# The order of the chosen experts: per-partition lists written whole by two indirect DMAs in place of 128 scatters of single values

## Chip, cores and metric

One NeuronCore of a Trainium2 chip runs the whole program. The metric is the device time of one execution in microseconds, as a median of several runs. Shares and durations inside the execution come from one profiled execution.

## What is computed

The program runs two transformer-like blocks over 256 tokens of width 2048 in float32 (16 meta tokens go ahead of them in the first block). The part that matters here is the expert layer of the first block: 8 heads, 128 by 128 product keys, 16,384 experts, 16 experts for each token and head.

```python
v1, i1 = lax.top_k(s1, K); v2, i2 = lax.top_k(s2, K)
cand = (v1[..., :, None] + v2[..., None, :]).reshape(B, L, PH, K * K)
cidx = (i1[..., :, None] * NK + i2[..., None, :]).reshape(B, L, PH, K * K)
top_s, pos = lax.top_k(cand, K)
idx = jnp.take_along_axis(cidx, pos, axis=-1)
gate = jax.nn.softmax(top_s, axis=-1)
...
u = U[ib]
h = jax.nn.gelu(jnp.einsum('thkd,td->thk', u, xb).astype(jnp.float32), approximate=False)
w = (gb * h).astype(xb.dtype)
return jnp.einsum('thk,thkd->td', w, V[ib])
```

An expert that no token chose adds nothing to the sum, so rows of `V` need to be read only for the chosen ones. With the inputs that are used, the 32,768 choices of the 256 tokens fall on 13,426 different experts.

## The kernel before

**Stages around the change.** Expert number e = 128 i + p stands in partition p at place i. (1) The queries are projected, scored against the keys, and `choose` (lines 865 to 881) finds each token's experts, head by head, with VectorE. It is a background generator: `bg.tick()` lets it go a step each time a piece of TensorE's work has been traced. Each head adds 32 indirect DMAs on GpSimd's queue (line 836, 256 in all), each of which adds 128 gate values at single places of `table`, a DRAM tensor of 16,384 experts by 256 tokens. (2) Meanwhile `hidden(e2)` (lines 741 to 756) works through all 64 pairs e2 of 128-expert groups: two loads of `peer_u` of 1 MB on SyncE's queue, split by ScalarE (line 176) and VectorE (line 177) into a high and a low part for three matmul passes, 96 matmuls in a pair, then the activation and a store to the DRAM tensor `hid` on ScalarE's queue (lines 753 to 755). (3) After the choice `compact` (lines 940 to 983) counts the used experts with TensorE, gives each expert its place (used ones first, in order of their number) and writes the numbers to the DRAM tensor `order` with 128 indirect DMAs of 128 single values of 4 bytes (line 972). It then loads `order` as `rows` (line 981). (4) When all 64 pairs have been traced, `index_rows` (lines 985 to 997) turns `rows` with TensorE, so that partition p and column k hold the expert at place 128 k + p. (5) A conditional (line 1086) holds the work for the case of more than 106 x 128 = 13,568 used experts (`NS` = 106). Its body is a unit: each engine that has work in it loads the count, compares and branches, and nothing behind it is traced among the work ahead of it. (6) `weigh` (line 999) gathers gates (`gq` from `table`) and activations (`hq` from `hid`) of 2 x 128 places by four indirect DMAs and multiplies them. Five pairs of `weigh` and the projections of the memory's keys and values (`mem_w_kv`, lines 1095 to 1110) come first. Then 106 rows of 128 experts are taken one after the other: `v_row` (line 1021) gathers 128 rows of 8 KB of `peer_v`, and 24 matmuls add them up (line 1115 on), the next pair's `weigh` being traced in between.

**What sets the order.** TensorE's order is written by hand. The other engines' queues are ordered by a scheduler, roughly by the order of tracing. GpSimd's queue is served in order, so line 972 stands behind the 256 instructions of line 836. `peer_u` loads go through 4 slots of `raw`, the split halves through 4 slots, `gq` and `hq` through 2. `memory()` (line 886, the norm of the memory's rows) is background work that starts at pair `MEM` = 40.

Of the kernel before, what the change touches and what calls it, by code (L numbers as in the profile page):

```python
# [8 lines left out]
F32 = mybir.dt.float32  # L9
# [11 lines left out]
NT = 256  # L21
# [53 lines left out]
def _build(tc, nc, V, S, T, G, ctx, I, out):  # L75
# [265 lines left out]
    table = tc.dram_tile([128 * 128 * NT, 1], F32, name="table")  # L341
# [3 lines left out]
    def zeros(x):  # L345

        z = cst.tile([128, 128], F32, name="zero", tag="zero", bufs=1)
        V.tensor_scalar(z.bitcast(I32), x.bitcast(I32), 0, None, op0=OP.bitwise_and)  # L348
        nc.gpsimd.dma_start(table.rearrange("(q p a b) o -> q p a (b o)", q=16, p=128, b=128)[next(zq)],  # L349
                            z[:, None, :].to_broadcast([128, 16, 128]))  # L350

# [588 lines left out]
    def compact(cnt):  # L940


        ev = tkp.tile([128, NR], I32, name="ev", bufs=1)
        G.iota(ev, pattern=[[128, NR]], base=0, channel_multiplier=1)
        rev = tkp.tile([128, NR], F32, name="rev", bufs=1)
        V.tensor_scalar(rev, ev, -1.0, 128.0 * NR, op0=OP.mult, op1=OP.add)
        order = tc.dram_tile([128 * NR, 1], I32, name="order")
        put = []
        sums = [tkp.tile([128, 64 + NR], F32, name=f"sums{i}", bufs=1) for i in range(2)]
        for x in sums:  # L950
            V.memset(x[:, :64], 0.0)
        used = tkp.tile([128, NR], F32, name="used", bufs=1)
        V.tensor_scalar(used, cnt, 0.5, None, op0=OP.is_gt)
        V.tensor_copy(sums[0][:, 64:], used)
        for i in range(7):
            x, y = sums[i % 2], sums[1 - i % 2]
            V.tensor_add(y[:, 64:], x[:, 64:], x[:, 64 - (1 << i):64 + NR - (1 << i)])
# [3 lines left out]
        T.matmul(p[:, :NR], lhsT=triu, rhs=used, start=True, stop=False)  # L961
        T.matmul(p[:, :NR], lhsT=ones, rhs=sums[1][:, 63:63 + NR], start=False, stop=True)
        T.matmul(p[:, NR:NR + 1], lhsT=ones, rhs=sums[1][:, 63 + NR:64 + NR], start=True, stop=True)
        yield
        ids["n"] = ixp.tile([128, 1], I32, name="count")
        V.tensor_copy(ids["n"], p[:, NR:NR + 1])
        mq = tkp.tile([128, NR], F32, name="mq", bufs=1)
        V.scalar_tensor_tensor(mq, used, -1.0, rev, op0=OP.add, op1=OP.mult)
        pos = tkp.tile([128, NR], I32, name="pos", bufs=1)
        V.scalar_tensor_tensor(pos, p[:, :NR], -1.0, mq, op0=OP.add, op1=OP.subtract)  # L970
        for k in range(NR):
            d = G.indirect_dma_start(
                out=order, out_offset=bass.IndirectOffsetOnAxis(ap=pos[:, k:k + 1].bitcast(U32), axis=0),
                in_=ev[:, k:k + 1], in_offset=None)
            for d0 in put:
                tc.declare_no_dep(d.ins, d0.ins, reason="other places")
            put.append(d)
            if k % 32 == 31:
                yield
        rows = tkp.tile([128, 128], I32, name="rows", bufs=1)  # L980
        nc.gpsimd.dma_start(rows, order.rearrange("(b p) o -> b (p o)", p=128))
        ids["rows"] = rows
        yield

    def index_rows():

        of = tkp.tile([128, 128], F32, name="of", bufs=1)
        with tc.issue_after(mark["V"].ins):
            V.tensor_copy(of, ids["rows"])
        p = ptp()  # L990
        T.transpose(p[:, :NR], of, ident)
        ids["g"] = ixp.tile([128, NR], I32, name="ig")
        ids["v"] = ixp.tile([128, 2, NR], I32, name="iv")
        with tc.issue_after(mark["V"].ins):
# [73 lines left out]
    for e2 in range(NR // 2):  # L1068
# [7 lines left out]
        for _ in hidden(e2):  # L1076
            bg.tick()
# [644 lines left out]
```

## Time and profile before

| what | us |
|---|---|
| median of 3 runs | 3613.2 |
| lowest and highest run | 3604.57, 3615.6 |
| the profiled execution | 3621.4 |
| its span, first to last instruction | 3619.4 |
| TensorE busy in the span | 3469.8 (96%) |
| VectorE busy | 2370.8 (66%) |
| ScalarE busy | 1624.5 (45%) |
| GpSimd busy | 1153.5 (32%) |

TensorE is busy nearly throughout, so the time is TensorE's work plus the stretches in which it waits or runs at a lower granted clock. The profiled execution is 8.2 us longer than the median of the runs. A share of the whole span says little here: each stage has its own limit, and the stretches have to be read one by one.

### The profile page before, as it was taken

Reading aid. Unit: us, or ns where it says so; the run is one execution under the profiler, and the core shown is the slowest. Engines: PE = TensorE matmul, PEld = TensorE weight load, DVE = VectorE, ACT = ScalarE, POOL = GpSimd, SP = SyncE. Lnnn points to the kernel's source line nnn. Section 1 sums busy time; section 2 is a strip of 40 time slices with the busy share of each in tenths; the row PEclk is TensorE's granted clock in tenths of the full one; section 3 lists DMA queues with packets and bytes.
Section 4 is the critical chain, followed back from the end, with each engine's and each line's share of the span. In section 5 each row is a group of like instructions: output and inputs, shape, how many; then the busy total and the mean of one; then the engine's idle time right before and its main releaser. Section 6 shows DMA issues by size and latency. Waiting matters only on the chain. (4 is left out here: it accounts for less than half of the span.)

```text
span 3619.4 us, 54532 instructions
## 1 busy us (share of the span) xinstructions
PE 3469.8 (96%) x21755; PEld 3099.8 (86%) x21755; DVE 2370.8 (66%) x4316; ACT 1624.5 (45%) x2148; POOL 1153.5 (32%) x780
## 2 busy tenths in 40 slices
PE   8999999999999999999986499999999999999999
PEld 7988899888889999999976378877777899999987
DVE  6975579976559996655422355544456688888875
ACT  6444443445454443344322254443336645454543
POOL 0000000000006888888645536666640000000000
PEclk9999999999999999999988799999999999999999
DMA  4544445667666777767896476666665444444443
GB/s 161 173 152 140 142 138 188 219 210 257 231 210 164 202 196 201 204 196 233 173 151 91 172 256 229 233 225 211 223 213 171 146 155 158 155 162 146 158 162 112
DMA packets 351878, 662.05 MB, mean 183 GB/s; under 512 B 60033, under 2 KB 209765, under 8 KB 321906
## 3 DMA queue, kind: packets, MB, share of 16 engines
q1 hardware_dynamic: 256962, 472.68, 42.2%
q0 software_dynamic: 75232, 164.85, 15.9%
q10 hardware_dynamic: 19424, 20.98, 1.9%
q8 instruction: 173, 2.83, 0.3%
q14 instruction: 87, 0.71, 0.1%
HBM read 620.43 MB, written 37.99 MB: 182 GB/s over the span
## 5 line engine op out<-in xcount | busy, mean ns | idle before, releaser
L176 ACT CAST hi<-raw 128x1024 fp32r<-128x1024 f32 x1093 | 1142.7, 1049 | 1669.6 <-PE acc L208 568.2
L177 DVE TENSOR_TENSOR lo<-raw,hi 128x1024 fp32r<-128x1024 f32 x1093 | 1327.6, 1222 | 775.1 <-ACT hi L176 763.9
L206 PE MATMUL mm<-xh,hi 128*128 128x256 f32 x2064 | 595.3, 288 | 23.1 <-ACT hi L176 22.5
L836 POOL DMA_INDIRECT table<-gts,idx x256 | 573.2, 2239 | 135.5 <-issue 75.6
L206 PE MATMUL acc<-xh,hi 128*128 128x256 f32 (+1 forms) x2048 | 604.9, 295 | 0.7 <-DVE hg L428 0.7
L208 PE MATMUL mm<-xh,lo 128*128 128x256 f32 x2064 | 593.4, 288 | 10.0 <-DVE lo L177 8.8
L207 PE MATMUL mm<-xl,hi 128*128 128x256 f32 x2064 | 591.3, 286 | 0.4 <-issue 0.4
L208 PE MATMUL acc<-xh,lo 128*128 128x256 f32 (+1 forms) x2048 | 586.8, 287 | 0.0
L207 PE MATMUL acc<-xl,hi 128*128 128x256 f32 (+1 forms) x2048 | 586.6, 286 | 0.0
L206 PEld LDWEIGHTS mm<-xh,hi 128*128 128x128 f32 x2064 | 402.7, 195 | 25.8 <-ACT hi L176 24.9
L208 PEld LDWEIGHTS mm<-xh,lo 128*128 128x128 f32 x2064 | 402.4, 195 | 14.1 <-DVE lo L177 12.2
L207 PEld LDWEIGHTS mm<-xl,hi 128*128 128x128 f32 x2064 | 402.8, 195 | 0.9 <-issue 0.8
L206 PEld LDWEIGHTS acc<-xh,hi 128*128 128x128 f32 x2048 | 390.5, 191 | 5.4 <-issue 5.0
L207 PEld LDWEIGHTS acc<-xl,hi 128*128 128x128 f32 x2048 | 390.8, 191 | 1.4 <-issue 1.0
L208 PEld LDWEIGHTS acc<-xh,lo 128*128 128x128 f32 x2048 | 389.9, 190 | 1.3 <-issue 1.2
L349 POOL DMA_DIRECT2D table<-zero x16 | 18.0, 1122 | 975.1 <-DVE zero L348 953.5
L206 PE MATMUL acc<-hi,xh 128*128 128x512 f32 x704 | 280.3, 409 | 0.0
L207 PE MATMUL acc<-lo,xh 128*128 128x512 f32 x704 | 278.2, 395 | 0.0
L208 PE MATMUL acc<-hi,xl 128*128 128x512 f32 x704 | 277.8, 395 | 0.0
L437 DVE SCALAR_TENSOR_TENSOR h<-hg,cw,h 128x256 f32<-128x256 f32 x480 | 203.7, 480 | 0.0
L736 POOL DMA_INDIRECT gq<-table,ig x106 | 152.3, 1437 | 149.3 <-DVE hq L1009 121.8
L207 PE MATMUL acc<-lo,wh 128*128 128x512 f32 x424 | 170.3, 402 | 13.3 <-DVE lo L177 13.3
(521 smaller groups left out, 5751.4 us busy)
## 6 DMA issues: line engine op xcount, KB each, us to landing
raw<-in_peer_u_dram SPq DMA_DIRECT2D x128, 1024.0 KB
raw<-in_w_in_dram SPq DMA_DIRECT2D x112, 1024.0 KB
raw<-in_dn_w_in_dram SPq DMA_DIRECT2D x88, 1024.0 KB
raw<-in_w_out_dram SPq DMA_DIRECT2D x48, 1024.0 KB
raw<-in_w_gla_out_dram SPq DMA_DIRECT2D x16, 1024.0 KB
table<-zero POOLq DMA_DIRECT2D x16, 1024.0 KB
raw<-in_w_conv_out_dram SPq DMA_DIRECT2D x16, 1024.0 KB
raw<-in_peer_wq_dram SPq DMA_DIRECT2D x16, 1024.0 KB
```

Source lines behind the costliest of these rows:

```text
L176: S.copy(hi, src)
L177: V.tensor_sub(lo, src, hi)
L206: T.matmul(o, lhsT=lh, rhs=rh, start=start, stop=False)
L207: T.matmul(o, lhsT=lh, rhs=rl, start=False, stop=False)
L208: T.matmul(o, lhsT=ll, rhs=rh, start=False, stop=stop)
L349: nc.gpsimd.dma_start(table.rearrange("(q p a b) o -> q p a (b o)", q=16, p=128, b=128)[next(zq)], z[:, None, :].to_broadcast([128, 16, 128]))
L437: V.scalar_tensor_tensor(ca[:, f], hg[:, f - f0, j:j + NT], w, ca[:, f], op0=OP.mult, op1=OP.add)
L736: G.indirect_dma_start(out=dst, out_offset=None, in_=rows, in_offset=bass.IndirectOffsetOnAxis(ap=ids.bitcast(U32), axis=0))
L836: d = G.indirect_dma_start(out=table, out_offset=bass.IndirectOffsetOnAxis(ap=idx[:, i, s:s + 1].bitcast(U32), axis=0), in_=gts[:, i, s:s ...
```

## The change

`compact` no longer gives each expert a place by a running sum over columns. Each partition makes a list of its own used experts (number + 1, falling, zeros behind) by 16 rounds of the 8 greatest values with VectorE. The 128 lists, 128 values or 512 bytes each, are written whole to DRAM at element offsets which follow from the counts of the partitions ahead. Two indirect DMAs do this, one for partitions 0 to 63 and one for 64 to 127 (each writes the other half to a spare area), into two buffers that two earlier DMAs have filled with zeros. The partitions take turns (0, 64, 1, 65, ...), so that the zeros at a list's end meet only the other half's place, and the two buffers are added after the load. If two neighbours in that order have fewer than 128 used experts together, 32,768 is added to the count. `got` is loaded as 128 x 106 directly, so partition p holds places 106 p to 106 p + 105, and the turn with TensorE goes. Places without an expert point at row 16,384, a zero row which `table` gets in addition; `hid` and `peer_v` are read there at row 16,383 (`ids["h"]`).

The conditional's body no longer goes on from place 13,568: it works through all 64 pairs in natural order with plain loads on SyncE's queue (the order is then all zero rows). `index_rows` is traced after pair `IX` = 55 and not after pair 63, and `MEM` is 30 and not 40.

The diff, with the removed bodies of `compact` and `index_rows` left out (they are printed above):

```diff
@@ -338,7 +338,7 @@
         split_store(xh[:, k], xl[:, k], xs, pcol(N1, k))
     pn1.close()
-    table = tc.dram_tile([128 * 128 * NT, 1], F32, name="table")
+    table = tc.dram_tile([(128 * 128 + 1) * NT, 1], F32, name="table")
     zq = iter(range(16))
@@ -346,8 +346,11 @@
         z = cst.tile([128, 128], F32, name="zero", tag="zero", bufs=1)
         V.tensor_scalar(z.bitcast(I32), x.bitcast(I32), 0, None, op0=OP.bitwise_and)
-        nc.gpsimd.dma_start(table.rearrange("(q p a b) o -> q p a (b o)", q=16, p=128, b=128)[next(zq)],
+        q = next(zq)
+        nc.gpsimd.dma_start(table[:128 * 128 * NT].rearrange("(q p a b) o -> q p a (b o)", q=16, p=128, b=128)[q],
                             z[:, None, :].to_broadcast([128, 16, 128]))
+        if q == 0:
+            nc.gpsimd.dma_start(table[128 * 128 * NT:].rearrange("(p b) o -> p (b o)", p=2), z[:2])
     pgl = ctx.enter_context(ExitStack())
@@ -940,72 +943,118 @@
     def compact(cnt):
...
+        lists = [tc.dram_tile([257 * 128, 1], F32, name=f"lists{i}") for i in range(2)]
+        z = tkp.tile([128, 129], F32, name="zl", bufs=1)
+        V.memset(z, 0.0)
+        for x in lists:
+            nc.gpsimd.dma_start(x[:129 * 128].rearrange("(p b) o -> p (b o)", p=128), z)
+        ev = tkp.tile([128, 3, NR], I32, name="ev", bufs=1)
+        G.iota(ev[:, 0], pattern=[[128, NR]], base=1, channel_multiplier=1)
+        G.iota(ev[:, 1], pattern=[[1, NR]], base=0, channel_multiplier=0)
+        G.iota(ev[:, 2], pattern=[[0, NR]], base=0, channel_multiplier=1)
+        evf = tkp.tile([128, 3, NR], F32, name="evf", bufs=1)
+        V.tensor_copy(evf, ev)
+        late = tkp.tile([128, 2, NR], F32, name="late", bufs=1)
+        V.tensor_scalar(late, evf[:, 1:], 63.5, -127.0, op0=OP.is_gt, op1=OP.mult)
+        rank = evf[:, 1:]
+        V.scalar_tensor_tensor(rank, rank, 2.0, late, op0=OP.mult, op1=OP.add)
+        low = tkp.tile([128, 1], F32, name="low", bufs=1)
+        V.tensor_scalar(low, late[:, 1, 0:1], -63.5, None, op0=OP.is_gt)
+        far, ahead = late[:, 0], late[:, 1]
+        V.tensor_sub(far, rank[:, 1], rank[:, 0])
+        V.tensor_scalar(ahead, far, -1.0, 0.5, op0=OP.mult, op1=OP.is_gt)
+        both = tkp.tile([128, NR], F32, name="both", bufs=1)
+        V.tensor_scalar(both, far, 0.5, 0.25, op0=OP.subtract, op1=OP.mult)
+        V.tensor_mul(both, both, both)
+        V.tensor_scalar(both, both, -1.0, -0.05, op0=OP.mult, op1=OP.is_gt)
+        mid = tkp.tile([128, 1], F32, name="mid", bufs=1)
+        V.tensor_scalar(mid, rank[:, 1, 0:1], -1.0, -126.5, op0=OP.mult, op1=OP.is_gt)
+        yield
+        keys = [tkp.tile([128, NR], F32, name=f"keys{i}", bufs=1) for i in range(2)]
+        used = keys[1]
         V.tensor_scalar(used, cnt, 0.5, None, op0=OP.is_gt)
...
+        cn = tkp.tile([128, 2], F32, name="cn", bufs=1)
+        V.tensor_reduce(cn[:, 0:1], used, axis=AX.X, op=OP.add)
+        V.tensor_mul(keys[0], used, evf[:, 0])
+        own = tkp.tile([128, NR], F32, name="own", bufs=1)
+        yield
+        for r in range(NR // 8):
+            r8 = slice(r * 8, r * 8 + 8)
+            V.max(own[:, r8], keys[r % 2])
+            if r < NR // 8 - 1:
+                V.match_replace(keys[1 - r % 2], in_to_replace=own[:, r8], in_values=keys[r % 2], imm_value=0.0)
+            if r % 4 == 3:
+                yield
         p = pmm()
-        T.matmul(p[:, :NR], lhsT=triu, rhs=used, start=True, stop=False)
-        T.matmul(p[:, :NR], lhsT=ones, rhs=sums[1][:, 63:63 + NR], start=False, stop=True)
-        T.matmul(p[:, NR:NR + 1], lhsT=ones, rhs=sums[1][:, 63 + NR:64 + NR], start=True, stop=True)
-        yield
+        T.matmul(p[:, 0:1], lhsT=ahead, rhs=cn[:, 0:1], start=True, stop=True)
+        T.matmul(p[:, 1:2], lhsT=both, rhs=cn[:, 0:1], start=True, stop=True)
+        off = tkp.tile([128, 3], F32, name="off", bufs=1)
+        V.tensor_scalar(off[:, 1:2], tok[:, 0:1], 128.0, 129.0 * 128, op0=OP.mult, op1=OP.add)
+        V.tensor_sub(off[:, 0:1], p[:, 0:1], off[:, 1:2])
+        V.tensor_mul(off[:, 2:3], low, off[:, 0:1])
+        to = [tkp.tile([128, 1], I32, name=f"to{i}", bufs=1) for i in range(2)]
+        V.tensor_add(to[0], off[:, 2:3], off[:, 1:2])
+        V.tensor_sub(to[1], p[:, 0:1], off[:, 2:3])
+        few = tkp.tile([128, 1], F32, name="few", bufs=1)
+        V.tensor_scalar(few, p[:, 1:2], -1.0, -127.5, op0=OP.mult, op1=OP.is_gt)
+        V.tensor_scalar(few, few, mid[:, 0:1], 32768.0, op0=OP.mult, op1=OP.mult)
+        V.tensor_add(cn[:, 1:2], cn[:, 0:1], few)
+        for x in range(2):
+            G.indirect_dma_start(
+                out=lists[x].rearrange("(p b) o -> p (b o)", b=128),
+                out_offset=bass.IndirectOffsetOnAxis(ap=to[x].bitcast(U32), axis=1), in_=own, in_offset=None)
+        yield
+        yield
+        p = pmm()
+        T.matmul(p[:, 0:1], lhsT=ones, rhs=cn[:, 1:2], start=True, stop=True)
         ids["n"] = ixp.tile([128, 1], I32, name="count")
...
+        V.tensor_copy(ids["n"], p[:, 0:1])
+        fit = tkp.tile([128, 1], F32, name="fit", bufs=1)
+        V.tensor_scalar(fit, p[:, 0:1], -1.0, -128.0 * NS - 0.5, op0=OP.mult, op1=OP.is_gt)
+        got = tkp.tile([128, 2, NS], F32, name="got", bufs=1)
+        for x in range(2):
+            nc.gpsimd.dma_start(got[:, x], lists[x][:128 * NS].rearrange("(p k) o -> p (k o)", p=128))
+        ids["got"], ids["fit"] = got, fit
         yield
     def index_rows():
-        of = tkp.tile([128, 128], F32, name="of", bufs=1)
+        got, fit = ids["got"], ids["fit"]
         with tc.issue_after(mark["V"].ins):
...
+            V.tensor_add(got[:, 0], got[:, 0], got[:, 1])
+        V.tensor_scalar(got[:, 0], got[:, 0], fit[:, 0:1], None, op0=OP.mult)
+        V.tensor_scalar(got[:, 1], got[:, 0], 0.0, 128.0 * 128 + 1, op0=OP.is_equal, op1=OP.mult)
+        ex = tkp.tile([128, NS], F32, name="ex", bufs=1)
+        V.scalar_tensor_tensor(ex, got[:, 1], -1.0, got[:, 0], op0=OP.add, op1=OP.add)
+        ids["g"] = ixp.tile([128, NS], I32, name="ig")
+        V.tensor_copy(ids["g"], ex)
+        V.tensor_scalar(ex, ex, 128.0 * 128 - 1, None, op0=OP.min)
+        ids["h"] = ixp.tile([128, NS], I32, name="ih")
+        V.tensor_copy(ids["h"], ex)
+        ids["v"] = ixp.tile([128, 2, NS], I32, name="iv")
+        for k in range(2):
+            V.tensor_scalar(ids["v"][:, k], ex, 2.0, float(k), op0=OP.mult, op1=OP.add)
+    def weigh(e2, wp, ww, natural=False):
         wh = wp.tile([128, 2, NT], F32R, name="wh")
         wl = wp.tile([128, 2, NT], F32R, name="wl")
         gq = ww.tile([128, 2, NT], F32, name="gq")
         hq = ww.tile([128, 2, NT], F32, name="hq")
-        for e in range(2):
-            k = e2 * 2 + e
-            fetch(gq[:, e], table.rearrange("(e t) o -> e (t o)", t=NT), ids["g"][:, k:k + 1])
-            fetch(hq[:, e], hid, ids["g"][:, k:k + 1])
+        if natural:
+            es = slice(e2 * 2, e2 * 2 + 2)
+            nc.sync.dma_start(gq, table[:128 * 128 * NT].rearrange("(i p t) o -> p i (t o)", p=128, t=NT)[:, es])
+            nc.sync.dma_start(hq, hid.rearrange("(i p) t -> p i t", p=128)[:, es])
+        else:
+            for e in range(2):
+                k = e2 * 2 + e
+                fetch(gq[:, e], table.rearrange("(e t) o -> e (t o)", t=NT), ids["g"][:, k:k + 1])
+                fetch(hq[:, e], hid, ids["h"][:, k:k + 1])
         V.tensor_mul(hq, hq, gq)
         split_store(wh, wl, hq)
         return wh, wl
@@ -1021,7 +1070,7 @@
     def v_row(k):
         raw = load(None, [2, 1024])
-        fetch(raw.rearrange("p h f -> p (h f)"), Vv, ids["g"][:, k:k + 1])
+        fetch(raw.rearrange("p h f -> p (h f)"), Vv, ids["h"][:, k:k + 1])
         return raw
     def add_row(a, e, w, hi, lo, start, stop):
@@ -1064,7 +1113,7 @@
     pge = ctx.enter_context(ExitStack())
     gel = pge.enter_context(pool("gel", bufs=4))
-    MEM = 40
+    MEM, IX = 30, 55
     for e2 in range(NR // 2):
         if e2 == MEM:
             pme = ctx.enter_context(ExitStack())
@@ -1075,8 +1124,10 @@
             bg.add(memory(), 0.75)
         for _ in hidden(e2):
             bg.tick()
+        if e2 == IX:
+            bg.drain()
+            index_rows()
     bg.drain()
-    index_rows()
     pge.close()
     ptk.close()
     pwt = ctx.enter_context(ExitStack())
@@ -1084,11 +1135,12 @@
     pww = pwt.enter_context(ExitStack())
     ww = pww.enter_context(pool("wtw", bufs=2))
     with tc.If(nc.values_load(ids["n"][0:1, 0:1]) > NS * 128):
-        for e2 in range(NS // 2, NR // 2):
-            w = weigh(e2, wp, ww)
+        for e2 in range(NR // 2):
+            w = weigh(e2, wp, ww, True)
             for hf in range(2):
                 a = [[acc() for _ in range(2)] for _ in range(2)]
-                for e, hi, lo in halved(v_rows(e2, hf), 2, 1024):
+                rows = Vv.rearrange("(i p) f -> p i f", p=128)[:, e2 * 2:e2 * 2 + 2, hf * 1024:hf * 1024 + 1024]
+                for e, hi, lo in halved(load(rows, [2, 1024]), 2, 1024):
                     add_row(a, e, w, hi, lo, e == 0, e == 1)
                 take_values(a, hf)
     ws = [weigh(e2, wp, ww) for e2 in range(WA)]
```

## Rows read from the trace of the kernel before

**Rows 1.** The page's 40 slices: TensorE's busy tenths.
```profile
PE   8999999999999999999986499999999999999999
```

**Rows 2.** Stretches: busy PE, PEld, DVE, ACT, POOL; clock, DMA share, GB/s.
```profile
1190.00:1753.00 563.00, 562.69 (x4801) 561.68 (x4800) 378.39 (x637) 247.59 (x276) 495.93 (x220) 1.00 0.73 206
1753.00:1977.00 224.00, 186.79 (x1346) 179.50 (x1344) 74.53 (x84) 64.41 (x76) 118.26 (x107) 0.90 0.91 136
1977.00:2038.00 61.00, 1.27 (x2) 0.47 (x2) 2.01 (x5) 2.52 (x3) 29.04 (x32) 0.50 0.18 40
...
2135.00:2400.00 265.00, 264.89 (x1135) 213.30 (x1136) 140.22 (x141) 113.43 (x122) 163.54 (x140) 1.00 0.68 235
2400.00:2650.00 250.00, 236.71 (x992) 184.48 (x992) 118.86 (x123) 98.02 (x104) 161.13 (x124) 1.00 0.63 219
```

**Rows 3.** Tile order: count, ns min/median/max, first and last start.
```profile
L972 POOL DMA_INDIRECT order<-ev,pos x128: 952/958/1964, 1760.0 to 2015.2; - x128
L981 POOL DMA_DIRECT2D rows<-order x1: 587/587/587, 2023.2 to 2023.2; - x1
```

**Rows 4.** The same for line 836, the additions into table.
```profile
L836 POOL DMA_INDIRECT table<-gts,idx x256: 1542/2370/7091, 1108.8 to 1757.1; - x128
```

**Rows 5.** Waits, 1760 to 2030 us: who waited for whom, us, times, longest.
```profile
ACT hi L176 <- DMA raw<-in_peer_u_dram: 123.4, 21, 10.2
...
DVE of L989 <- DMA rows<-order: 49.2, 1, 49.2
```

**Rows 6.** DMA queues, 1300 to 1740 us: packets, MB, share of 16 engines.
```profile
q1 hardware_dynamic: 11033, 80.29, 53.5%
q0 software_dynamic: 24624, 0.10, 12.5%
```

**Rows 7.** DMA queues, 1780 to 1960 us.
```profile
q1 hardware_dynamic: 3067, 22.26, 88.5%
...
q0 software_dynamic: 2724, 0.05, 1.5%
```

**Rows 8.** Stores of the activated pairs from 1740 us on.
```profile
L755 ACTq DMA_DIRECT2D hid<-gel x16: 366/366/367, 1743.1 to 1977.6; - x16
```

**Rows 9.** VectorE's timeline, pairs 47 and 48: start, us, what.
```profile
1730.13 0.69 DVE L753 TENSOR_TENSOR gel<-mm,rB 128x512 f32<-128x512 f32 x1 [0.70 <-PE mm L208]
...
1741.65 0.69 DVE L753 TENSOR_TENSOR gel<-mm,rB 128x512 f32<-128x512 f32 x1 [0.69 <-PE mm L208]
```

**Rows 10.** Line 1086, the branch, by sequencer.
```profile
L1086 ACTq TENSOR_LOAD <-count x1: 470/470/470, 1978.0 to 1978.0; - x1
...
L1086 PEldq TENSOR_LOAD <-count x1: 491/491/491, 2026.3 to 2026.3; - x1
...
L1086 PEldq COMPARE_BRANCH  x1: 3361/3361/3361, 2026.9 to 2026.9; - x1
...
L1086 DVEq EVENT_SEMAPHORE  x1: 21/21/21, 2030.5 to 2030.5; - x1
```

**Rows 11.** The chain that ended last, behind the branch.
```profile
2030.62 5.11 DMA raw<-in_mem_w_kv_dram
...
2038.18 0.80 PE acc L207
```

**Rows 12.** VectorE's timeline among the chosen rows: two successive products.
```profile
2502.49 0.69 DVE L1009 TENSOR_TENSOR hq<-hq,gq 128x512 f32<-128x512 f32 x1 [6.16 <-DMA hq<-hid,ig]
...
2514.57 0.69 DVE L1009 TENSOR_TENSOR hq<-hq,gq 128x512 f32<-128x512 f32 x1 [6.25 <-DMA hq<-hid,ig]
```

**Rows 13.** GpSimd's timeline there: a pair's last activation gather.
```profile
2510.69 0.95 POOL L736 DMA_INDIRECT hq<-hid,ig  x1 [0.30 <-issue]
```

**Rows 14.** DMA, 2140 to 2700 us: gathers' queue, gathers of peer_v.
```profile
q0 software_dynamic: 23392, 123.58, 64.1%
...
raw<-in_peer_v_dram,ig POOLq DMA_INDIRECT x88
```

**Rows 15.** Groups on VectorE by shape, 1050 to 1800 us: busy us, mean ns.
```profile
L768 DVE MAX8 tv<-w 128x8 f32<-128x128 f32 x32 | 9.1, 285 | 0.0
```

More of the change, by code (lines that the diff above doesn't have):

```diff
@@ L940, in compact @@
     def compact(cnt):
[L943 to L951, printed above, removed]
@@ L952, in compact @@
-        used = tkp.tile([128, NR], F32, name="used", bufs=1)
-        V.tensor_scalar(used, cnt, 0.5, None, op0=OP.is_gt)
[L954 to L957, printed above, removed]
+        lists = [tc.dram_tile([257 * 128, 1], F32, name=f"lists{i}") for i in range(2)]
+        z = tkp.tile([128, 129], F32, name="zl", bufs=1)
+        V.memset(z, 0.0)
@@ L960, in compact @@
         p = pmm()
-        T.matmul(p[:, :NR], lhsT=triu, rhs=used, start=True, stop=False)
-        T.matmul(p[:, :NR], lhsT=ones, rhs=sums[1][:, 63:63 + NR], start=False, stop=True)
-        T.matmul(p[:, NR:NR + 1], lhsT=ones, rhs=sums[1][:, 63 + NR:64 + NR], start=True, stop=True)
-        yield
+        T.matmul(p[:, 0:1], lhsT=ones, rhs=cn[:, 1:2], start=True, stop=True)
         ids["n"] = ixp.tile([128, 1], I32, name="count")
-        V.tensor_copy(ids["n"], p[:, NR:NR + 1])
-        mq = tkp.tile([128, NR], F32, name="mq", bufs=1)
@@ L968, in compact @@
[L968 to L979, printed above, removed]
@@ L980, in compact @@
-        rows = tkp.tile([128, 128], I32, name="rows", bufs=1)
-        nc.gpsimd.dma_start(rows, order.rearrange("(b p) o -> b (p o)", p=128))
-        ids["rows"] = rows
+        V.tensor_copy(ids["n"], p[:, 0:1])
[4 more added lines that the diff above has]
+            nc.gpsimd.dma_start(got[:, x], lists[x][:128 * NS].rearrange("(p k) o -> p (k o)", p=128))
@@ L983, in compact @@
+        ids["got"], ids["fit"] = got, fit
         yield
     def index_rows():
-        of = tkp.tile([128, 128], F32, name="of", bufs=1)
+        got, fit = ids["got"], ids["fit"]
         with tc.issue_after(mark["V"].ins):
[L989 to L994, printed above, removed]
-            V.tensor_copy(ids["g"], p[:, :NR])
-            for k in range(2):
-                V.tensor_scalar(ids["v"][:, k], p[:, :NR], 2.0, float(k), op0=OP.mult, op1=OP.add)
@@ L999, in weigh @@
-    def weigh(e2, wp, ww):
+            V.tensor_add(got[:, 0], got[:, 0], got[:, 1])
[5 more added lines that the diff above has]
+        V.tensor_copy(ids["g"], ex)
```

## The prediction

> **What bounds the kernel now.** I read the page's slices first: TensorE is at nine tenths or more nearly everywhere, with one hole a little behind the middle, digits 8, 6, 4 and 9 [rows 1]. So the time is TensorE's work plus that hole, and only the hole can be won. The stretches around it come next [rows 2]. From 1190 to 1753 us, where `hidden` runs beside the choice, TensorE is busy for 562.69 of 563 us at the full clock. From 1753 to 1977 us the same `hidden` work gets 186.79 of 224 us, the granted clock falls to 0.90 of full speed, and the DMA engines' share rises from 0.73 to 0.91 while they move 136 and not 206 GB/s. From 1977 to 2038 us TensorE does 1.27 us of work in 61, at the lower clock level (0.50 of full, 1.2 GHz).
>
> The instructions on `order` explain where this begins and ends [rows 3]: the 128 scatters start at 1760.0 us, right behind the last addition to `table` at 1757.1 [rows 4], and the last of them starts at 2015.2; the load of `rows` follows at 2023.2. In this time ScalarE waits 123.4 us for `peer_u` loads, and VectorE, at the end, 49.2 us for `rows` [rows 5]. The DMA queues say how: from 1300 to 1740 us the loads on q1 take 53.5% of 440 us for 80.29 MB, 2.93 us of all 16 engines for 1 MB; from 1780 to 1960 us it is 88.5% of 180 us for 22.26 MB, 7.16 us for 1 MB [rows 6, 7]. The scatters' own packets show only 1.5% there [rows 7], but a load of 1 MB costs 2.4 times as much beside them. A pair needs two, 14.3 us, against 11.52 us of TensorE's time for it (next part): the loads become the bound. I take the scatters as the cause, since the change of pace falls on their start. The additions to `table`, also of 4 bytes each, do not have this effect (2.93 us).
>
> **The change part by part.** *Hidden stretch.* The 128 scatters go. Two indirect DMAs and two loads of `got` take their place, issued at about 1760 us, since the 256 additions ahead of them on GpSimd stay. The last 16 stores of pairs span 1743.1 to 1977.6 us, 15 intervals in 234.5 us [rows 8]. Undisturbed pairs are 11.52 us apart (1730.13 to 1741.65) [rows 9], so the 15 would take 172.8 us. Gain 61.7 us. The slowed clock of this stretch is within it and is not counted again. What might stay of the slowing is the part of 512-byte rows: 256 rows for 16,384 single values; by count that is 61.7 x 256/16,384 = 1 us at most, by bytes (131 KB for 66 KB) it would be twice the old loss, but both DMAs land in a few us and the queues then hold only `peer_u`. I take 0, range 0 to 5.
>
> Here a rule of the Trainium skill bears: DMA: Bandwidth & Descriptors, Specifications, says that a transfer under 512 bytes makes the DMA engine read, modify and write. By that rule alone the additions to `table` should have slowed `peer_u` as the scatters did, and the new rows of 512 bytes would not. The trace agrees with the second half at most: additions 2.93 us, scatters 7.16 us for 1 MB, so the size is not the whole cause. By the rule the rest of the slowing is 0, by the count above 1 us.
>
> *The hole.* The chain now is: last scatter 2015.2, its landing and `rows` at 2023.2, the turn, and only then TensorE reaches the conditional at 2026.3, needs 3.36 us for the branch, VectorE passes at 2030.5, and the first `mem_w_kv` load starts at 2030.6 [rows 3, 10, 11]. It takes 5.1 us, the split some 2.4, and matmuls start at 2038.18 [rows 11]. ScalarE had reached the conditional at 1978.0, behind the last store [rows 10]. The last matmul of `hidden` ends near 1976.2 (the last store's 1977.6 less 1.4 us: a product of 0.69 [rows 9] and an activation of like size). The hole is 62.0 us. After the change nothing on TensorE's or VectorE's queue stands between the last pair and the conditional. What stays is count and branch on TensorE, 2026.3 to 2030.5, 4.2 us, then from 2030.5 to 2038.2, 7.7 us: 11.9 us. The body is now 64 pairs long and not 11, so the other engines' branches may take as long as TensorE's 3.36 us; SyncE, which now has the body's loads, may wait for the last stores. Neither is shown; I bound them by 3.4 us for the one and 8.0 us (scatter to landing, 2015.2 to 2023.2 [rows 3]) for the other. Below 11.9: with the first load ahead of the branch it would be 4.2. I take 12, range 4 to 24. Gain 50 us, range 38 to 58.
>
> *Index work moved to pair 55.* `got` must have landed when VectorE comes to `index_rows`. Lists issued at 1760, landed 8.0 us later, `got` 3.1 us after that (2023.2 to 2026.3 [rows 3, 10]): near 1773 us, with two loads in a row 1775. Pair 55's product follows that of pair 48 (1741.65) by seven intervals, 1822. There are 47 us to spare, so this wait costs nothing; past that each us late stops the split halves of `peer_u`, and TensorE behind them, for one. The same holds for `memory()`, ten pairs earlier, and for its four loads on SyncE's queue: the stretch has 27% of DMA time free [rows 2].
>
> *VectorE.* 16 rounds of MAX8 at 285 ns and 15 replacements of about the same size [rows 15] are 8.8 us, and some 35 short operations of at most 0.3 us are 10 us more; eight or so go. All of it falls into 1050 to 1830 us, where VectorE is busy 378.39 of 563 us [rows 2], a third free. Uncovered it would cost 19 us; TensorE lost 0.3 us in this stretch beside the larger work of the choice, so I take 1, range 0 to 5.
>
> *Gathers in a new order.* Before, a gather's 128 rows lay close together (rising expert numbers, about four fifths of a contiguous 1 MB of `peer_v`). Now partition p takes place 106 p + k of lists that fall by 128, and neighbouring rows lie hundreds of KB apart over 134 MB. Number and size of the rows are the same. No row of this trace shows a gather of distant 8 KB rows. The gathers' queue moves 123.58 MB in 64.1% of 560 us, 2.90 us for 1 MB [rows 14], as much as the contiguous `peer_u` loads (2.93). So the pace looks like that of the engines, not of the place in memory. I take no change, bounded above by the only slowed load in the trace, a factor of 2.4, and below by 0.
>
> *Sum.* 61.7 + 50 - 1 = 110.7, say 110 us. On the profiled execution that is 3621.4 - 110 = 3511; taken from the median 3613.2 it is **3503 us**. The profiled execution stands 8.2 us over the median, and the gain lies in waits that any execution has. The likeliest case's own range is 3490 to 3525.
>
> **The rivals.** *Slow gathers (ends slower).* Among the chosen rows VectorE's product waits 6.2 us in each pair for `hq`, and the pairs are 12.08 us apart [rows 12], beside 11.2 us of pure matmul time (48 matmuls, where 1135 fill 265 us [rows 2]). `hq` is issued at 2510.69 and used at 2514.57: 2.9 us behind the end of the issue [rows 13, 12]. So the loop gq, row, hq, product already hangs on landing times, and each us more in landing is a us for each of 53 pairs. The DMA time of a pair is 64.1% of 560 us over 44 pairs, 8.2 us [rows 14]. With a factor f on the gathers the pair grows by 2.9 (f - 1) us while 8.2 f stays under it. At f = 1.2: 0.6 x 53 = 31 us, 3534. At f = 1.7: 2.0 us x 53 = 108 us, and the gain is gone; above, slower than before. At 2.4, 19.7 us of DMA time for a pair: 53 x 7.6 = 400 us, 3903. For it: the loop has no slack in its second half (236.71 of 250 us [rows 2]). Against: equal cost of gathers and contiguous loads now.
>
> The Trainium skill, HBM Reference, Latency, puts an access at 0.2 us on average and 2 us under high load. By that, were distant rows to meet the loaded case, landing would grow by up to 1.8 us, near the point where the gain is gone. No run here shows it yet.
>
> *The scatters were not the cause.* `peer_u` stays slow for another reason at the end of `hidden`; only the hole is won: 3613 - 49 = 3564. Against it: the start at 1760.
>
> *A new wait.* The lists come late (a wait on GpSimd's queue that the trace has not got), VectorE stands at pair 55: at 47 + 30 us late, 3533.
>
> *The natural order runs.* If the count passed 13,568 or two neighbours held under 128, 64 pairs at 12.08 us come in addition, 773 us: 4276. Against it: 13,426 experts are used; by the reference's choice the least sum of two neighbours is 162.
>
> **How the numbers follow.** Chances: forecast 0.72; slow gathers short of the turning point 0.09, past it 0.04; scatters not the cause 0.07; new wait 0.05; natural order 0.03. Left out of the range are the last, gathers past the turning point and the scatters' case (0.14). The range is 3490 to 3550. A difference under 0.3%, 11 us, is about what can't be told from no change. Faster 0.91, same 0.02, slower 0.07.
>
> **What would show it.** Right: pairs 11.5 us apart up to the last, 1 MB of `peer_u` near 2.9 us to the end, the last store near 1916 us, TensorE idle some 12 us behind it, pairs of chosen rows still near 12 us. Wrong: a stop of VectorE at pair 55; a conditional that holds SyncE's first load until long after the last store; `hq` landing later than 2.9 us, or a gathers' queue well over 64%.

## The result, and the profile after

| what | before | after |
|---|---|---|
| median of 4 runs, us | 3608.89 | 3504.52 |
| lowest and highest run, us | 3602.95, 3615.6 | 3497.31, 3509.83 |
| ratio of the times, 95% interval | | 0.9709, 0.9681 to 0.9737 |
| the profiled execution, us | 3621.4 | 3497.31 |
| its span, us | 3619.4 | 3495.4 |

The change wins 104 us by the medians, and the 3503 us of the prediction are 1.5 us from the median. The two profiles lie further apart than the medians, by 124 us: that of before shows an execution slower than all four of its runs, that of after the shortest of four. Where a gain is read from these two profiles alone, it is that pair's gain; other executions are set beside it below.

The page's slices of TensorE after the change (busy tenths, answering [rows 1]) have one 8 left where 8, 6, 4 and 9 stood:

```profile
PE   8999999999999999999998999999999999999999
```

The stretches, as in [rows 2] (busy us of PE, PEld, DVE, ACT and POOL with their counts, granted clock, DMA share, GB/s):

```profile
1190.00:1753.00 563.00, 562.24 (x4796) 561.24 (x4795) 387.29 (x693) 250.85 (x286) 495.78 (x221) 1.00 0.73 209
1753.00:1914.00 161.00, 159.92 (x1333) 159.72 (x1331) 75.92 (x76) 61.86 (x67) 9.02 (x6) 1.00 0.52 175
1914.00:1926.40 12.40, 0.80 (x1) 0.29 (x1) 1.22 (x2) 2.31 (x3) 5.34 (x6) 0.53 0.59 208
```

From 1753 us on, TensorE now works 159.92 of 161 us at the full clock (before 186.79 of 224 at 0.90), and the DMA share is 0.52 and not 0.91. VectorE has 9 us more to do ahead of that (387.29 for 378.39), and TensorE is busy for 0.45 us less there. The tiles by name (count, ns min/median/max, first and last start), answering [rows 3] and [rows 8]:

```profile
L758 ACTq DMA_DIRECT2D hid<-gel x64: 366/366/393, 1174.2 to 1914.3; - x64
...
L1007 POOL DMA_INDIRECT lists<-own,to x2: 975/1497/2019, 1758.5 to 1760.8; - x2
L1020 POOL DMA_DIRECT2D got<-lists x2: 577/586/594, 1765.3 to 1765.9; - x2
...
L1029 DVE TENSOR_TENSOR got<-got x1: 257/257/257, 1821.4 to 1821.4; 128x106 f32<-128x106 f32 x1
```

The lists go out at 1758.5 and 1760.8, their load is issued at 1765.9, and its first use is at 1821.4, 56 us later. VectorE's timeline shows the last two pairs still 11.52 us apart, as in [rows 9]:

```profile
1901.44 0.69 DVE L756 TENSOR_TENSOR gel<-mm,rB 128x512 f32<-128x512 f32 x1 [0.70 <-PE mm L208]
1912.96 0.69 DVE L756 TENSOR_TENSOR gel<-mm,rB 128x512 f32<-128x512 f32 x1 [9.33 <-PE mm L208]
```

The branch by sequencer, as in [rows 10], and the chain of waits behind it (start us, us, what), as in [rows 11]:

```profile
L1137 SPq EVENT_SEMAPHORE  x8: 17/17/17, 1886.2 to 1918.7; - x8
...
L1137 PEldq COMPARE_BRANCH  x1: 3386/3386/3386, 1911.2 to 1911.2; - x1
...
L1137 ACTq TENSOR_LOAD <-count x1: 473/473/473, 1914.8 to 1914.8; - x1
L1137 ACTq COMPARE_BRANCH  x1: 50/50/50, 1915.3 to 1915.3; - x1
...
L1137 ACTq EVENT_SEMAPHORE  x1: 17/17/17, 1918.4 to 1918.4; - x1
```

```profile
1918.97 5.03 DMA raw<-in_mem_w_kv_dram
...
1924.10 1.05 ACT hi L176
...
1925.18 1.24 DVE lo L177
...
1926.46 0.80 PE acc L207
```

TensorE takes its branch while the last pair's sum still goes through VectorE and ScalarE. ScalarE comes to the conditional behind the last store, passes at 1918.4, SyncE at 1918.7, and the first `mem_w_kv` load starts at 1918.97. Two things run side by side here. ScalarE's branch is recorded with 0.05 us at 1915.3, but its next step comes 3.1 us later; before the change it came after 0.5 us:

```profile
L1086 ACTq COMPARE_BRANCH  x1: 45/45/45, 1978.5 to 1978.5; - x1
L1086 ACTq EVENT_SEMAPHORE  x1: 17/17/17, 1979.0 to 1979.0; - x1
```

And SyncE waits in the conditional for the last store of `hid`, which the body would read: the store's packets end at 1917.98, and SyncE's wait on that store's semaphore passes at 1918.44. The load starts behind the later of the two; e11 below shows them in the other order.

Where the two profiles differ, stage by stage (the first stores start at 1176.2 and 1174.2, 2.0 us earlier after):

| stage | from and to what | before | after | won |
|---|---|---|---|---|
| hidden pairs | first to last store | 801.4 | 740.1 | 61.3 |
| hole | last store to the chain's first matmul behind the branch | 60.6 | 12.2 | 48.4 |
| memory's projections | to the first product of the chosen rows | 96.9 | 97.4 | -0.5 |
| chosen rows | first to last product | 617.4 | 604.7 | 12.7 |
| the rest | to the end of the span | 866.9 | 866.8 | 0.1 |

With the 2.0 us at the start this makes the 124 us. The 12.7 us of the chosen rows were not forecast; the experiments take them up.

### The profile page after: what moved, and what is told of

Its sections match the earlier page's. It is cut to its first block, busy times and chain, and to the rows that moved or that the text cites. A ratio compares the mean times of both kernels' runs of the same rounds, so it can differ in the third digit from the quotient of the medians.

```text
span 3495.4 us, 54464 instructions
## 1 busy us (share of the span) xinstructions
PE 3426.1 (98%) x21754; PEld 3080.0 (88%) x21754; DVE 2386.8 (68%) x4376; ACT 1626.7 (47%) x2148; POOL 1031.5 (30%) x660
## 5 line engine op out<-in xcount | busy, mean ns | idle before, releaser
L206 PE MATMUL mm<-xh,hi 128*128 128x256 f32 x2064 | 586.2, 284 | 0.8 <-DVE fit L1017 0.8
L207 PE MATMUL mm<-xl,hi 128*128 128x256 f32 x2064 | 583.9, 283 | 0.0
L208 PE MATMUL mm<-xh,lo 128*128 128x256 f32 x2064 | 583.8, 283 | 0.0
L206 PEld LDWEIGHTS mm<-xh,hi 128*128 128x128 f32 x2064 | 394.9, 191 | 0.9 <-issue 0.8
L207 PEld LDWEIGHTS mm<-xl,hi 128*128 128x128 f32 x2064 | 395.0, 191 | 0.1
L208 PEld LDWEIGHTS mm<-xh,lo 128*128 128x128 f32 x2064 | 394.9, 191 | 0.0
```

The lines of the kernel that those rows point to most:

```text
L206: T.matmul(o, lhsT=lh, rhs=rh, start=start, stop=False)
L207: T.matmul(o, lhsT=lh, rhs=rl, start=False, stop=False)
L208: T.matmul(o, lhsT=ll, rhs=rh, start=False, stop=stop)
```

## Experiments

The chips of the three groups differ, and each kernel is compared with the kernel before on its own chip: e1 to e4 (median of before 3588.29 us), e5, e6, e7 and e9 (3606.92), e8, e10 and e11 (3596.97). A ratio is estimated from all times of both kernels and is not the quotient of the two medians. Single times have no interval; of those kernels the profile is what counts.

**The kernel before once more (e3), an unchanged copy, line numbers one higher.**

> The kernel before once more, for a second profile. Matmuls of 512 columns among the chosen rows took 396 ns before and 389 ns after the change, 19 us over 106 rows. If this belongs to the kernel (where its tiles lie), this profile shows 396 ns again. If it belongs to the single execution, it may show 389 ns, and the stage is then some 12 us shorter.

One time, 3597.86 us. Its tiles `order` and `gel`, then its DMA queues from 1780 to 1940 us (packets, MB, share of 16 engines):

```profile
L973 POOL DMA_INDIRECT order<-ev,pos x128: 952/958/1908, 1760.2 to 1995.3; - x128
...
L756 ACTq DMA_DIRECT2D hid<-gel x64: 366/367/395, 1174.6 to 1950.1; - x64
```

```profile
q1 hardware_dynamic: 2850, 20.72, 82.3%
```

Its matmuls of 512 columns take 396 ns again (shown under e9), so that time belongs to the kernel. The slowing is there again, 160 x 0.823 / 20.72 = 6.36 us for 1 MB (7.16 in [rows 7]), but the scatters take 235 us here and 255 us in [rows 3], and the hidden pairs 775.5 us and not 801.4. The memory's projections start at 2018.2, 22.9 us behind the start of the last scatter; in the first profile it is 23.0 us (2015.2 and 2038.18). So in the kernel before it is the end of the scatters that sets this point, and each us by which they spread less takes one from what their removal wins. What the stretch and the hole lose is one sum, 92 us in this execution and 112 in the first (2018.2 and 2038.18 less 1926.46).

**Single scatters side by side, back in the kernel after (e4).** Nothing waits for them, and they stand behind the loads of `got`.

```diff
+        at = ...  # iota: 128 k + p
+        for k in range(64):
+            G.indirect_dma_start(out=order, out_offset=bass.IndirectOffsetOnAxis(ap=at[:, k:k + 1], axis=0),
+                                 in_=own[:, k:k + 1], in_offset=None)
```

> The changed kernel, and 64 scatters of 128 single values each to 64 KB / 2 of DRAM side by side, as those of before but half as many, put behind the loads of the lists. Nothing reads them. My theory: from about 1767 us they slow the loads of peer_u for some 64 x 2 us = 128 us, pairs come 14 to 17 us apart and not 11.5, the last store comes 25 to 40 us later (near 1945 us), the hole stays at 12 us, the time is about 3535 us. Rival, the scatters are not the cause: the pairs stay at 11.5 us and the time at 3505 us.

One time, 3510.28 us. DMA from 1770 to 1880 us, then the tiles:

```profile
q1 hardware_dynamic: 2258, 16.43, 89.8%
...
raw<-in_peer_u_dram SPq DMA_DIRECT2D x17, 1024.0 KB, 22.5
```

```profile
L1028 POOL DMA_INDIRECT order<-own,at x64: 952/958/1980, 1768.5 to 1888.9; - x64
...
L758 ACTq DMA_DIRECT2D hid<-gel x64: 366/366/393, 1175.3 to 1928.1; - x64
```

The loads of `peer_u` take 6.01 us for 1 MB (110 x 0.898 / 16.43); without the scatters the same window of the kernel after holds 19.90 MB at 52.0%, 2.87 us. A load lands after 22.5 us and not 4.9. So the scatters alone bring the slowing of the loads back, and "the scatters were not the cause" has fallen. The price of these 64, 752.8 - 740.1 = 12.7 us, is half of the lowest expected: at 6.0 us a pair's two loads (2.1 MB) take 12.6, only 1.1 over the 11.52 of TensorE's time, and the train covers some ten pairs (120 us).

**The same number of rows of 512 bytes (e5), and single values 512 bytes apart (e6).**

```diff
+        order = tc.dram_tile([8192, 128], F32, name="order")      # e5: in_=own[:, :]
+        G.iota(at, pattern=[[128 * 128, 64]], base=0, channel_multiplier=128)   # e6: 4 bytes each 512
```

> The changed kernel with 64 indirect DMAs of 128 rows of 512 bytes each behind the loads of the lists, in place of the 64 scatters of single values of the run before; as many DMAs and rows, 4.2 MB and not 33 KB. Beside the single values 1 MB of peer_u took 6.2 us of all engines' time (2.9 alone) and the last store came 14 us later. Theory size (a write under 512 bytes is what costs): 1 MB takes under 3.5 us and the last store comes 0 to 4 us later than in the changed kernel. Theory pace (number of small pieces, of whatever size): 6 us for 1 MB, and the last store 14 us or more later.

> The same 64 scatters of single values, but each value 512 bytes from the next and not 4, over 4 MB. Theory closeness (single values side by side in one stretch of DRAM hinder each other): 1 MB of peer_u takes about 3 us as beside the additions to table, whose places lie far apart, and the last store does not move by more than 3 us. Theory size or pace: 6 us for 1 MB and the last store 14 us later, as with the values side by side.

One time each, 3502.97 and 3513.34 us. DMA from 1770 to 1880 us and then the tiles, of e5 and after it of e6:

```profile
q1 hardware_dynamic: 2785, 20.33, 55.1%
```

```profile
L1028 POOL DMA_INDIRECT order<-own,at x64: 954/1102/1437, 1768.9 to 1859.4; - x64
...
L758 ACTq DMA_DIRECT2D hid<-gel x64: 366/366/393, 1176.5 to 1916.7; - x64
```

```profile
q1 hardware_dynamic: 2796, 20.42, 53.3%
```

```profile
L1028 POOL DMA_INDIRECT order<-own,at x64: 954/1104/1437, 1768.2 to 1858.7; - x64
...
L758 ACTq DMA_DIRECT2D hid<-gel x64: 366/367/393, 1175.8 to 1916.0; - x64
```

Neither slows anything: 2.98 and 2.87 us for 1 MB, and the hidden pairs take 740.2 us in both. The scatters themselves are done in 90 us and not 120. e6 has the count and the size of e4; only the places differ. So neither the number of the values nor their 4 bytes is the cause; that they lie close together is. Two things change at once in that: each value's distance to the next (4 or 512 bytes) and the whole stretch that is written (32 KB or 4 MB). The runs do not tell these apart.

**Side by side, but slower (e7).** As e4, with two iotas of GpSimd ahead of each scatter.

```diff
+            for _ in range(2):
+                last = G.iota(ev, pattern=[[1, 3 * NR]], base=0, channel_multiplier=0)
```

> The 64 scatters of single values side by side, each behind two iota instructions on GpSimd, so one in some 3 us as with the additions to table and not one in 1.9 us. Theory pace: peer_u takes 3 to 4 us for 1 MB and the last store moves by under 4 us. Theory closeness or size: each scatter still costs what it did, so 1 MB takes 5 us or more, and with scatters up to the end of the hidden stage the last store comes 10 us or more later.

One time, 3524.32 us. DMA from 1770 to 1880 us and the tile `order`:

```profile
q1 hardware_dynamic: 2309, 16.88, 89.8%
```

```profile
L1031 POOL DMA_INDIRECT order<-own,at x64: 974/981/2017, 1773.9 to 1921.6; - x64
```

Spread over 148 us and not 120, they still make 1 MB cost 5.85 us (6.01 in e4). The last store is at 1926.2, 752.9 us behind the first, as in e4. A pace a fifth lower does not help. The 3 us for each scatter that the run aimed at were not reached, it is 2.3 us (147.7 us for 64); the additions to `table`, which slow nothing, come every 2.5 us (1108.8 to 1757.1 us for 256, [rows 4]).

**Index work last (e1).**

```diff
-    MEM, IX = 30, 55
+    MEM, IX = 30, 63
```

> The changed kernel with the index work traced behind pair 63, not behind pair 55; all else as changed. My theory: the lists are in the chip by about 1775 us, so nothing is gained by the earlier place but the ten short VectorE instructions, some 2.5 us, which now stand between the last product and the conditional. The hole between the last store and the first matmul of the memory's projection grows from 12 us to 14 or 15 us, the time by 2 to 4 us over the changed kernel. Rival: it is the earlier place that closed the hole; then it is 50 to 60 us again and the time about 3553 us.

3505.66 us, ratio 0.9745 (0.9695 to 0.9795). The index work now starts at 1914.3 on VectorE; the last store is at 1915.1 and the memory's projections begin at 1927.6, a hole of 12.5 us for 12.2. The 2 to 3 us of the theory are not seen in the hole; in the time, whose interval is 36 us wide, they could not be. The place at pair 55 brings nothing that can be measured, since the hole is the way through the conditional and the first load, and VectorE's short steps lie beside it.

**Distant rows in the kernel before (e2).** Partition p takes the places 106 p + k of the old order, and the turn goes. The conditional's body, which is not entered, is renumbered and stays 11 pairs long.

```diff
-        nc.gpsimd.dma_start(rows, order.rearrange("(b p) o -> b (p o)", p=128))
+        nc.gpsimd.dma_start(rows, order[:128 * NS].rearrange("(p k) o -> p (k o)", p=128))
...
-            V.tensor_copy(ids["g"], p[:, :NR])
+            V.tensor_copy(ids["g"][:, :NS], ids["rows"])
```

> The kernel before, with its 128 scatters, but the order is loaded as partition p, places 106 p to 106 p + 105, without the turn on TensorE. So a gather's 128 rows lie some 106 experts apart and no longer side by side: the gather order alone is changed. My theory: the pairs of chosen rows stay at 12.0 to 12.1 us in their second half, the time is that of the kernel before within 8 us. Rival, slow gathers: the queue of the gathers goes clearly over 64% of the engines' time, pairs grow by 0.6 us or more each, and the time by 30 us or more.

3599.34 us, ratio 1.0015 (0.9994 to 1.0037), so at most 13 us more, where the rival asked for 30 or more. The gathers' queue from 2140 to 2600 us, e2 and then e3:

```profile
q0 software_dynamic: 18751, 102.35, 64.0%
```

```profile
q0 software_dynamic: 18738, 102.33, 64.3%
```

The same bytes in the same share, and the chosen rows take 615.8 us beside 615.2 in e3. Places all over 134 MB cost no more than neighbours; "slow gathers" has fallen.

**The address of the products' tile (e9).** Among the chosen rows a matmul of 512 columns takes 389 ns after and 396 before, although its shape is the same. By the program's layout, which no profile shows, the tiles `wh` and `wl` had moved from byte 138,784 of a partition to 139,008, a multiple of 256. An unused tile of 224 bytes makes that move alone in the kernel before:

```diff
+        ixp.tile([128, 56], I32, name="gap")
```

> The kernel before with 224 unused bytes behind the count, which moves the weights of the chosen rows (wh, wl: what TensorE holds while the rows stream) to the addresses that they have in the changed kernel: 139,008 and not 138,784, a multiple of 256 and not 32 more. In profiles so far matmuls of 512 columns among the chosen rows took 396 ns in each kernel with the old address and 389 ns in each with the new one. Theory address: 389 ns here too, the stage of the chosen rows is 8 to 15 us shorter and so is the time. Rival (the gathers' order or the lists make the difference): 396 ns, and the time is that of the kernel before within 5 us.

3605.27 us, ratio 0.9992 (0.9979 to 1.0005). The tile `wh` and, in a second fence, the stretch of the chosen rows in e9, then both for e3:

```profile
L206 PE MATMUL tp<-hi,wh x212: 389/389/496, 2123.3 to 2700.7; 128*128 128x512 f32 x106
```

```profile
2123.00:2739.00 616.00, 587.16 (x2555) 475.65 (x2554) 311.04 (x318) 255.12 (x280) 362.26 (x291) 1.00 0.65 223
```

```profile
L207 PE MATMUL tp<-hi,wh x212: 395/396/498, 2113.7 to 2689.8; 128*128 128x512 f32 x106
```

```profile
2114.00:2729.00 615.00, 600.05 (x2555) 476.78 (x2554) 312.76 (x316) 254.28 (x278) 357.07 (x291) 1.00 0.65 223
```

The address was the matter, since of what the gap moves TensorE reads only `wh` and `wl` here: the matmuls have 13 us less to do. But the stage stays as long, 616.0 us, and TensorE's 13 us are idle time, with VectorE's waits for `hq` longer (231.8 us over 2120 to 2700, 211.3 in e3). So it is not the matmuls that bound the stage, by the waits it is the gathers' loop, and the address alone explains none of the 12.7 us.

**A third slot for the gathers (e8), and the kernel after once more (e11).**

```diff
-    ww = pww.enter_context(pool("wtw", bufs=2))
+    ww = pww.enter_context(pool("wtw", bufs=3))
```

> The changed kernel with three slots and not two for gq and hq. In all profiles so far the pairs of chosen rows come 12 us apart in the second half of their stage, though 48 matmuls take 10.9 us (389 ns kind) or 11.2 us (396 ns kind): VectorE's product waits for hq, and the next gq gather waits for that product. My theory: this loop bounds the half, and is why moved weights gained nothing (616.0 us of stage beside 617.4). With a third slot a pair's gathers are issued a pair earlier, the waits for hq fall from 170 to 240 us to under 60 us, the stage from some 602 to 618 us to 580 to 595 us, and the time by 10 to 25 us over the changed kernel. Rival: the pace of the gathers themselves bounds it (their queue is at 63%); then nothing changes by more than 4 us.

> The changed kernel once more, for a comparison on the same chip as the two runs beside it and for a second interval. Ratio to the kernel before between 0.967 and 0.976; the stage of the chosen rows between 602 and 618 us as in the profiles so far.

e8 3499.6 us, 0.9723 (0.9681 to 0.9764); e11 3504.3 us, 0.9744 (0.9706 to 0.9783): not to be told apart, where 10 to 25 us less were expected of e8. The chosen rows take 608.5 and 612.2 us, and VectorE's waits for `hq` from 2020 to 2600 us come to 207.2 and 216.2 us, not to under 60. GpSimd's timeline in e8, one pair:

```profile
2452.42 1.69 POOL L739 DMA_INDIRECT gq<-table,ig  x1 [4.02 <-DVE hq L1058]
2454.41 1.43 POOL L739 DMA_INDIRECT gq<-table,ig  x1 [0.30 <-issue]
2456.15 1.96 POOL L739 DMA_INDIRECT raw<-in_peer_v_dram,ih  x1 [0.30 <-issue]
2458.42 0.95 POOL L739 DMA_INDIRECT hq<-hid,ih  x1 [0.31 <-issue]
```

The `gq` gather still waits for the product of an earlier pair, now 4.0 us, and the product (2451.46, then 2463.43) still for `hq`. A third slot does not loosen the loop of 12 us, so the theory of the two slots has fallen. Why a gather with a slot more still waits for a product was not found, and what holds the loop, GpSimd's fixed order or the slots of `raw`, was not separated. The kernel after has now been profiled in e11 as well, and its rows took 7.5 us more than in the first profile. Over all profiles in which the loop itself is as in one of the two kernels, the rows of after take 602.4 to 617.9 us (seven with e1, e4 to e7 and e11, mean 610.5), those of before 615.2 to 617.4 (four with e2, e3 and e9, mean 616.1). So about half of the 12.7 us is the spread of executions, and whether the other 6 belong to the change is open.

In e11 SyncE passes the conditional ahead of ScalarE (last store 1914.3, its packets end at 1916.27, SyncE's wait for them passes at 1916.66), and the first load starts at 1917.85, right behind ScalarE:

```profile
L1138 SPq EVENT_SEMAPHORE  x8: 17/17/17, 1886.1 to 1916.9; - x8
...
L1138 ACTq EVENT_SEMAPHORE  x1: 17/17/17, 1917.8 to 1917.8; - x1
```

**The first load ahead of the branch (e10).** As e8, with the natural order's loads on GpSimd's queue with slots of their own, so that SyncE has no loads in the conditional.

```diff
-                for e, hi, lo in halved(load(rows, [2, 1024]), 2, 1024):
+                raw = nat.tile([128, 2, 1024], F32, name="natrow")
+                nc.gpsimd.dma_start(raw, rows)
+                for e, hi, lo in halved(raw, 2, 1024):
```

> As the run with three slots, and the conditional's body loads on GpSimd's queue into slots of its own, so that four loads of mem_w_kv are issued on SyncE's queue ahead of the conditional. My theory: of the hole of 12 us behind the last store, the wait for SyncE to pass and the 5 us of the first load go; 4 to 7 us are left for branch and split. Time 5 to 8 us under that of three slots alone. Rival: ScalarE's and VectorE's own passing of the conditional sets the hole, and it stays at 10 us or more.

3510.75 us, ratio 0.9763 (0.9726 to 0.98); e11 has 0.9744. Expected were 5 to 8 us less than e8's 3499.6 us; it is 11 us more, and no run of the one lies among those of the other (3504.57 to 3512.49 and 3485.59 to 3502.76). The chain of waits, then windows behind it:

```profile
1918.76 1.05 ACT hi L176
...
1919.83 1.24 DVE lo L177
...
1921.11 0.79 PE acc L207
```

```profile
1941.00:1961.00 20.00, 15.10 (x59) 10.79 (x57) 10.87 (x19) 7.02 (x10) 15.70 (x15) 0.90 0.64 218
1961.00:1981.00 20.00, 17.06 (x59) 12.61 (x59) 11.87 (x30) 10.28 (x14) 11.59 (x11) 0.76 0.53 178
```

The hole shrinks as forecast, to 6.2 us (last store 1914.9): ScalarE passes at 1918.5 and splits a load that has already landed. But the projections behind it take 110 us and not 97: TensorE is idle for 8 us in these 40 and runs at 0.90 and 0.76 of the clock, where the kernel after is busy 39.35 of the same 40 us at 1.00. The 6 us were given back, and more. By the waits, SyncE's and GpSimd's loads meet there (a `raw` gather waits 13.1 us for a `mem_w_kv` load), and which of the two costs the projections their time was not isolated.

## Why the prediction came out right, point by point

- **Hidden stretch, 61.7 us forecast.** The pair of profiles gives 61.3. The cause is shown: e4 brings the slowed loads back, e5 and e6 do not. The size is that of one execution: e3 lost 35 us (775.5 less 740), and 64 of the 128 scatters cost 12.7 us in e4. The 14.3 us for a pair's two loads take a load of 1,048,576 bytes for 1 MB; it is 15.0, nearer the 15.6 us at which the pairs came (234.5 / 15).
- **The hole, 62 to 12 us.** The forecast counts from the last matmul, 1.4 us ahead of the last store, the table above from the store. Counted as in the forecast it is 13.6 us (1926.46 less 1912.9), and 48.4 us are won for 50. Behind the store come 4.7 us through the conditional to the load, 5.0 of loading and 2.5 to the first matmul. The 4.7 us are not the 4.2 us of the forecast, which were TensorE's count and branch: these lie beside the last pair's tail now. The two doubts that the forecast put at 0, bounded by 3.4 and 8.0 us, are real: ScalarE's next step comes 3.1 us behind its branch, and SyncE waits for the last store to land. They run side by side and took the place of the term that went, so that this sum came out is in part luck.
- **The sum, 110 us, was some 6 us too high for the median's 104.** It subtracts from the median, 3613.2, what one profiled execution lost, and that was the slowest: its scatters took 255 us, those of e3, e2 and e9 235 to 245.5. The remark that the gain lies in waits that any execution has was right in kind and not in size. The median of before itself fell by 4.3 us with a fourth run, which covers most of this. On e3's execution the two parts come to 91 us and not 110 (1174.6 to 2018.2, less the 752.3 us from 1174.2 to 1926.46). So the mechanism was right, the size depended on which execution was profiled, and that the forecast lies within 1.5 us is luck.
- **Index work at 0.** Used 56 us after issue; e1 shows no gain from its place, and the rival "a new wait" did not come up.
- **VectorE, 1 us.** TensorE was busy for 0.45 us less in the stretch of the lists; what of it is VectorE's was not isolated.
- **Gather order, 0.** e2 shows it within 13 us, and after the change the gathers' queue from 1980 to 2540 us moves 121.78 MB in 63.4%, 2.92 us for 1 MB against 2.90 [rows 14]. The Trainium skill (HBM Reference, Latency) puts an access under high load at ten times the average; nothing in e2 shows distant rows to be such a case.
- **Rows of 512 bytes, 0.** e5 shows it with 64 of them. The prediction held that size was not the whole cause. e6 goes further: the rule of the Trainium skill (DMA: Bandwidth & Descriptors, Specifications) on transfers under 512 bytes covers e4 and e6 alike, and only e4 slows other loads. By itself it would not have told the scatters from the additions to `table`, which are single values far apart (`table` has 256 values for each expert).
- **Missed.** The 12.7 us of the chosen rows in the profiles; and of the expectations, the price in e4 (a load only a little slower than TensorE costs only the difference), the slots in e8, in e9 that a faster matmul would shorten a stage that gathers bound, and in e10 the time.

Open: why values side by side slow the loads (the runs vary the places, not the part of the memory or of the engines that holds them up), whether their distance or the small stretch does it, what ScalarE's 3.1 us behind its branch are, what holds the pairs of the chosen rows at 12 us, and whether their stage is some us shorter after the change.

## What to carry to other kernels

When bulk loads go slow, look at the small writes that run beside them and at their places: single values side by side in DRAM cost another queue half its pace here (6.01 us for 1 MB and not 2.87), and rows of 512 bytes, or single values spread out, next to nothing (2.98 and 2.87). Where a late train of small transfers and a hole follow one another, cost them as one sum, up to the point where the next stage starts, and take it from more than one execution. Before an engine's work is shortened or a hole closed, see what bounds the stage behind: here 13 us of matmul time and 6 us of the hole were won and did not shorten the run.

## What the hardware showed beyond that

- Values of 4 bytes written side by side: 1 MB on another queue at 5.85 to 7.16 us (e7, [rows 7]); 512 bytes apart 2.87 (e6); rows of 512 bytes 2.98 (e5).
- A matmul of 512 columns took 396 ns (e3), and 389 ns when an unused tile moved what TensorE holds during it by 224 bytes (e9), by the program's layout from byte 138,784 of a partition to 139,008.
- A branch around a body that is not entered took 3.3 to 5.4 us on TensorE's sequencer in twelve of the thirteen profiles and 11.6 us in e2. On ScalarE it is recorded with 0.05 us, but the next step came 2.6 to 5.0 us behind it where the body is 64 pairs long (nine profiles) and 0.4 to 0.5 us behind it where it is 11 (four).
- Behind the idle hole of the kernel after, TensorE's matmuls take 0.43 us each at a granted clock of 0.50, the lower level (1.2 GHz), up to 1931.9 us; from 1932.21 on they take 0.23 us at 1.00.
